# Seven-product groups of a decoder layer: common parts seeded in the accumulator banks, and four chunks in four more groups

## The chip, the cores and the metric

The kernel runs on one core of a Trainium2 chip. The metric is the device time of one execution in microseconds. A core has a matrix engine (TensorE, PE in the profile; its weight loads are PEld), a vector engine (VectorE, DVE), a scalar engine (ScalarE, ACT), GpSimd (POOL) and a sync engine (SyncE, SP) that here issues the loads of the weights. Each engine works through its own queue in order, and engines wait for one another by semaphores. Matmuls write accumulator banks in PSUM, which VectorE and ScalarE can reach as well as SBUF.

## What is computed

One decoder layer on 256 tokens with a model width of 2048, everything in float32. Three token mixers (gated linear attention, stick-breaking attention, cross-attention into 256 memory tokens) are merged by sigmoid gates, projected, and followed by a SwiGLU FFN of width 5632. Cut to what matters here:

```python
proj = rmsnorm(x, attn_norm) @ w_in              # (256, 2048) @ (2048, ...), gates among it
...
g = jax.nn.sigmoid(gates.reshape(B, T, 3, D))
merged = g[:, :, 0] * y_gla + g[:, :, 1] * y_sb + g[:, :, 2] * y_mem
x = x + merged @ w_o
h2 = rmsnorm(x, ffn_norm)
gate, up = jnp.split(h2 @ w_gate_up, 2, axis=-1)
x = x + (jax.nn.silu(gate) * up) @ w_down
```

## The kernel before

**Split numbers.** To keep float32 accuracy, every operand is held as two rounded parts, high and low. A product of a 128x128 piece of activations and a 128x512 piece of weights is three matmuls: high by high, high by low, low by high (L235, L237 and L238 in the helper `mm`, L201 to L203 in `gemm`). Activations are split once. Weights arrive as float32 blocks of four chunks (a chunk is 128 rows by 512 columns, a block 1 MB) by a load that SP issues (L229, L189), and are split two chunks at a time by `split`: ScalarE casts the high part (L136, 128x1024), VectorE subtracts it from the raw data to get the low part (L137). The pairs of high and low tiles come from rings that `widen` makes: four pairs from the start, one more before the gates, one more before the FFN, so five and then six; a split waits until the matmuls that read the pair's last contents are done. Raw blocks have three buffers and later five.

**Plain products.** `gemm` computes 256 tokens by 512 columns: for two chunks, one split and 12 matmuls (two token tiles, two chunks, three matmuls).

**Seven-product groups.** `sgemm` computes 256 tokens by two blocks of 512 columns at once, into four accumulator banks `o[t, j]` (token tile t, column block j). The first eight chunks of the contraction are two halves of four (`SP`), so operand and weights are 2x2 matrices of blocks; for the first `p` chunks of each half (p is 2 or 4) the eight block products are replaced by seven, in the Winograd form of Strassen's scheme. The weight blocks are called 11, 12 (first half, column blocks 0 and 1) and 21, 22 (second half). The sums of weight blocks are made in place in the raw buffers by VectorE (L251, two chunks at a time) just ahead of the split; the sums of operand blocks are made once per operand by `make_forms` (L356) in the background. The products are

- `p1`: block 21 into a scratch bank x0; kept (L268, ScalarE copies x0 to an SBUF piece);
- `p2`: block 11, and `p3`: block 12, each straight into one accumulator bank;
- `p5`: 21 + 22 into a second scratch bank x1;
- `p6`: into x0 on top of p1; kept; `p7`: into x0 on top of both; kept, and then two subtractions from x1 by VectorE (L303, L304) give the kept parts of the other two banks;
- `q4`: a last sum into an accumulator bank.

A product of two chunks needs one split for only 6 matmuls. What the seven products do not cover is done plainly by `rest`, two chunks at a time with 12 matmuls per split: the rest of each half (`l`, only for p = 2) and the chunks from eight on (`r0` for column block 0, `r1` for 1; four steps each with 16 chunks). At the end each bank is added to its kept part by VectorE (L346, in `result`); where the caller passes `plus` (a residual), VectorE has added that to the kept part first (L306).

The steps of a group are called in an order written out by hand (`seq`, L330 and L332); one order for groups whose operand forms come late (`late`, the first group of the gates, of w_o and of gate_up), one for the others. The tile framework then lays out every engine's queue from that program, and lets an instruction move ahead where an earlier one would still wait. `step()` lets background work (transposing results into the next operand, making forms) move on after each split.

There are 22 such groups: 4 for two of the three gates (p = 4, each followed by two plain products and a merge), 2 for w_o (p = 2), 11 for gate/up (i = 0 to 10; p = 4 for odd i, else 2) and 5 for w_down (p = 2 where n0 is 0, else 4). The FFN is done in three parts (i = 0 to 3, 4 to 7, 8 to 10): gate/up groups, then w_down groups on what they gave; in the first two parts those add their result to DRAM by a DMA that POOL issues (L1032). The last part has 12 chunks, and all but its first 1024 columns are plain products. Each gate/up group ends with an activation on ScalarE (L984) and a multiplication on VectorE (L988); its result is transposed by TensorE (L390) and split during the group behind. The forms for w_down are made during i = 2, 6 and 10.

Of the kernel before, what the change touches and what calls it, by code (L numbers as in the profile page):

```python
# [18 lines left out]
D = 2048  # L19
KD = D // P  # L20
NB = 512
# [56 lines left out]
def trunk(ctx: ExitStack, tc: tile.TileContext, a, out):  # L78
# [129 lines left out]
    def sgemm(xs, forms, w, blks, p, row0=0, late=False, plus=None):  # L208
# [36 lines left out]
        def prod(dst, left, b, last, *sums, gone=()):  # L245


            for g in range(0, p, 2):
                for to, of in sums:
                    x, y = (q[i][0][:, g : g + 2] for i in (to, of))  # L250
                    dve.tensor_tensor(x, x, y, op=ALU.add)  # L251
                wh, wl = half(q[b][0], g)
                for i in range(2):
                    mm(dst, left[g + i], wh[:, i], wl[:, i], last and g + i == p - 1)
                if g + 2 == p:
                    for i in gone:
                        q[i][1]()
                step()
# [7 lines left out]
        def keep(at):  # L266
            c[at] = piece()
            act.copy(c[at][:], x0[:])  # L268
# [5 lines left out]
        def p1():  # L274
            fetch(21, 0, SP)
            prod(x0, single(1, 0), 21, False)
            keep((0, 0))
# [5 lines left out]
        def p3(last):  # L283
            fetch(12, 1, 0)
# [40 lines left out]
        w21, w22, w11, w12 = (  # L325
            [(f,), *((rest, j, k + g) for g in range(p, SP, 2))]
            for f, j, k in ((p1, 0, SP), (p5, 1, SP), (p2, 0, 0), (p3, 1, 0))
        )
# [5 lines left out]
        todo = [into.get(f[0], [(t, f[1]) for t in range(2)] if len(f) > 1 else []) for f in seq]  # L334
        done = []
        for n, (f, *args) in enumerate(seq):
            left = {at for later in todo[n + 1 :] for at in later}
            last = [at for at in todo[n] if at not in left]
            f(*args, *([last] if args else [bool(last)] if f in into else []))
            for j in range(2):  # L340
                if j not in done and (1, 1) in c and not {(0, j), (1, j)} & left:
                    done.append(j)
# [569 lines left out]
    for b, w_br in ((1, "w_br_sb"), (0, "w_br_gla")):  # L912
        if b == 0:
            flush()
        xo = pairs((o_gla, o_sb)[b])
        for n0 in range(0, D, 2 * NB):
            gs = []
            k = (b * D + n0) // NB
            for _, result in sgemm(xs, sx, a["w_gate"], (k, k + 1), 4, late=b == 1 and n0 == 0):
                gs.append([result(t) for t in range(2)])  # L920
                for t in range(2):
                    act.activation(gs[-1][t], gs[-1][t], AF.Sigmoid, scale=r_x[:, t : t + 1])
# [21 lines left out]
    for n0 in range(0, D, 2 * NB):  # L944
# [4 lines left out]
        plus = {(t, j): xr[j][:, t] for t in range(2) for j in range(2)}  # L949
        for j, result in sgemm(ms, sm_, a["w_o"], (n0 // NB, n0 // NB + 1), 2, late=n0 == 0, plus=plus):  # L950
# [3 lines left out]
            for t in range(2):  # L954
                v = result(t, x2[:, t, n : n + NB])
# [21 lines left out]
    for part in (range(0, 4), range(4, 8), range(8, NF)):  # L977
        fs, tiles = [], []
        for i in part:
            for j, result in sgemm(hs, sf, a["w_gate_up"], (i, NF + i), 4 if i % 2 else 2, late=i == 0):  # L980
                if j == 0:
                    g = [result(t) for t in range(2)]
                    for t in range(2):
                        act.activation(g[t], g[t], AF.Silu, scale=r2[:, t : t + 1])  # L984
                    continue
                u = [result(t) for t in range(2)]
                for t in range(2):
                    dve.scalar_tensor_tensor(u[t], u[t], r2[:, t : t + 1], g[t], op0=ALU.mult, op1=ALU.mult)  # L988
# [14 lines left out]
        def stored(n, result, width=NB):  # L1003
            for t in range(2):
                for c in range(0, NB, width):
                    v = result(t, slice(c, c + width))
                    nc.sync.dma_start(out[t * P : (t + 1) * P, n + c : n + c + width], v)

        for n0 in range(0, D, 2 * NB):
            if final and n0 > 0:  # L1010
                for n in (n0, n0 + NB):
                    o = gemm(fs, a["w_down"], n, row0=4 * part[0])

                    def summed(t, cols):
                        v = x2s[t][:, n + cols.start : n + cols.stop]
                        dve.tensor_tensor(v, v, o[t][:, cols], op=ALU.add)
                        return v


                    stored(n, summed, NB // 2 if n + NB == D else NB)  # L1020
                continue
            plus = None
            if final:
                plus = {(t, j): x2s[t][:, n0 + j * NB : n0 + (j + 1) * NB] for t in range(2) for j in range(2)}
# [55 lines left out]
```

## Time and profile before

| | |
|---|---|
| median of 3 runs | 1661.63 us (1660.17 to 1662.98) |
| the profiled execution | 1660.39 us |
| its span, first to last instruction | 1658.6 us |
| instructions | 19253, of them 7398 matmul and transpose instructions on PE |
| gate/up and w_down stage | from about 956 us to the end |
| TensorE clock granted | full (1.0) in the span |

All sums are made against the profiled execution, whose own time is 1.8 us longer than its span. Busy time is a union of rows: the rows of matmuls overlap their neighbours, so a mean duration is not what one instruction takes from the engine; the distance between starts is. A timeline merges neighbouring instructions of one kind into a row with a count. In lists of waits the first name is who waited, the second who ended the wait.

### The profile page before, as it was taken

Reading aid. Unit: us, or ns where it says so; the run is one execution under the profiler, and the core shown is the slowest. Engines: PE = TensorE matmul, PEld = TensorE weight load, DVE = VectorE, ACT = ScalarE, POOL = GpSimd, SP = SyncE. Lnnn points to the kernel's source line nnn. Section 1 sums busy time; section 2 is a strip of 40 time slices with the busy share of each in tenths; the row PEclk is TensorE's granted clock in tenths of the full one; section 3 lists DMA queues with packets and bytes.
Section 4 is the critical chain, followed back from the end, with each engine's and each line's share of the span. In section 5 each row is a group of like instructions: output and inputs, shape, how many; then the busy total and the mean of one; then the engine's idle time right before and its main releaser. Section 6 shows DMA issues by size and latency. Waiting matters only on the chain.

```text
span 1658.6 us, 19253 instructions
## 1 busy us (share of the span) xinstructions
PE 1647.8 (99%) x7398; PEld 1352.2 (82%) x7398; DVE 1287.8 (78%) x1510; ACT 927.6 (56%) x1121; POOL 20.6 (1%) x32
## 2 busy tenths in 40 slices
PE   9999999999999999999999999999999999999998
PEld 7888888888877887888888888888888888888887
DVE  6756566664664669987997899997979997979984
ACT  7654454664644456555555666665656565556552
POOL 0000000000000000000000000000000000000000
PEclk9999999999999999999999999999999999999999
DMA  9765345445444557457456645565775556774572
GB/s 338 264 232 199 132 173 177 156 164 188 153 153 150 180 182 272 157 185 261 152 187 232 238 181 205 208 225 198 218 247 177 204 185 220 207 248 178 189 270 79
DMA packets 53757, 330.24 MB, mean 199 GB/s; under 512 B 5905, under 2 KB 10513, under 8 KB 15521
## 3 DMA queue, kind: packets, MB, share of 16 engines
q1 hardware_dynamic: 49968, 320.17, 54.0%
q0 software_dynamic: 3232, 8.39, 2.5%
q8 instruction: 58, 0.95, 0.2%
q10 hardware_dynamic: 464, 0.45, 0.1%
q14 instruction: 35, 0.28, 0.0%
HBM read 320.60 MB, written 8.39 MB: 198 GB/s over the span
## 4 chain that ended last, share of the span: by engine, by line
PE 94%; DVE 4%; DMA 1%; ACT 1%; issue 0%; ACTq 0%; DVEq 0%
PE acc L238 13%; PE acc L237 13%; PE acc L235 13%; PE acc L201 13%; PE acc L203 13%; PE acc L202 13%; PE tmp L237 3%; PE tmp L238 3%; PE tmp L235 3%; DVE wl L137 2%; PE tmp L390 2%; DVE raw L251 1%; DVE cv L356 1%; DMA raw<-in_w_gate_up 0%; ACT wh L136 0%; PE tmp L621 0%
## 5 line engine op out<-in xcount | busy, mean ns | idle before, releaser
L136 ACT CAST wh<-raw 128x1024 fp32r<-128x1024 f32 (+1 forms) x686 | 714.9, 1051 | 637.5 <-PE acc L203 284.5
L137 DVE TENSOR_TENSOR wl<-raw,wh 128x1024 fp32r<-128x1024 f32 (+1 forms) x686 | 824.6, 1219 | 283.6 <-ACT wh L136 278.2
L201 PE MATMUL acc<-wh,xTh 128*128 128x512 f32 x576 | 230.3, 400 | 0.0
L203 PE MATMUL acc<-wh,xTl 128*128 128x512 f32 x576 | 225.0, 391 | 0.0
L202 PE MATMUL acc<-wl,xTh 128*128 128x512 f32 x576 | 224.6, 390 | 0.0
L235 PE MATMUL acc<-wh,hh 128*128 128x512 f32 x512 | 200.0, 391 | 0.0
L238 PE MATMUL acc<-wh,hl 128*128 128x512 f32 x512 | 199.5, 390 | 0.0
L237 PE MATMUL acc<-wl,hh 128*128 128x512 f32 x512 | 199.4, 389 | 0.0
L251 DVE TENSOR_TENSOR raw<-raw 128x1024 f32<-128x1024 f32 x132 | 159.9, 1219 | 5.0 <-DMA raw<-in_w_gate_up 3.1
L203 PEld LDWEIGHTS acc<-wh,xTl 128*128 128x128 f32 x576 | 108.1, 188 | 23.4 <-issue 0.3
L201 PE MATMUL acc<-wh,oh 128*128 128x512 f32 x320 | 126.1, 396 | 0.8 <-ACT oh L139 0.8
L201 PEld LDWEIGHTS acc<-wh,xTh 128*128 128x128 f32 x576 | 108.3, 188 | 22.0 <-issue 1.4
L202 PE MATMUL acc<-wl,oh 128*128 128x512 f32 x320 | 125.7, 393 | 0.5 <-DVE wl L137 0.5
L202 PEld LDWEIGHTS acc<-wl,xTh 128*128 128x128 f32 x576 | 108.3, 188 | 21.7 <-issue 0.7
L203 PE MATMUL acc<-wh,ol 128*128 128x512 f32 x320 | 125.5, 392 | 0.0
L237 PEld LDWEIGHTS acc<-wl,hh 128*128 128x128 f32 x512 | 96.2, 188 | 20.1 <-DVE wl L137 0.3
L238 PEld LDWEIGHTS acc<-wh,hl 128*128 128x128 f32 x512 | 96.1, 188 | 20.0
L235 PEld LDWEIGHTS acc<-wh,hh 128*128 128x128 f32 x512 | 96.2, 188 | 19.6
L235 PE MATMUL acc<-wh,fh 128*128 128x512 f32 x220 | 85.9, 391 | 0.1
L237 PE MATMUL acc<-wl,fh 128*128 128x512 f32 x220 | 85.6, 389 | 0.0
L238 PE MATMUL acc<-wh,fl 128*128 128x512 f32 x220 | 85.5, 389 | 0.0
L201 PEld LDWEIGHTS acc<-wh,oh 128*128 128x128 f32 x320 | 60.6, 189 | 15.5 <-ACT oh L139 1.7
(291 smaller groups left out, 2203.7 us busy)
## 6 DMA issues: line engine op xcount, KB each, us to landing
raw<-in_w_gate_up SPq DMA_DIRECT2D x88, 1024.0 KB, 5.0
raw<-in_w_in SPq DMA_DIRECT2D x72, 1024.0 KB, 4.9
raw<-in_w_down SPq DMA_DIRECT2D x44, 1024.0 KB, 4.9
raw<-in_w_gate SPq DMA_DIRECT2D x32, 1024.0 KB, 4.9
raw<-in_w_o SPq DMA_DIRECT2D x16, 1024.0 KB, 4.9
raw<-in_w_mem_kv SPq DMA_DIRECT2D x15, 1024.0 KB, 5.0
raw<-in_w_br_mem SPq DMA_DIRECT2D x8, 1024.0 KB, 5.1
raw<-in_w_br_sb SPq DMA_DIRECT2D x8, 1024.0 KB, 6.9
```

The costliest lines, as they stand in the source:

```text
L136: act.copy(hi, src)
L137: dve.tensor_tensor(lo, src, hi.bitcast(F32), op=ALU.subtract)
L201: pe.matmul(o[t][:], xh[:, s], wh[:, j], start=k == 0, stop=False)
L202: pe.matmul(o[t][:], xh[:, s], wl[:, j], start=False, stop=False)
L203: pe.matmul(o[t][:], xl[:, s], wh[:, j], start=False, stop=k == nk - 1)
L235: pe.matmul(dst[:], xh, wh, start=id(dst) not in begun, stop=False, skip_group_check=True)
L237: pe.matmul(dst[:], xh, wl, start=False, stop=False, skip_group_check=True)
L238: pe.matmul(dst[:], xl, wh, start=False, stop=last, skip_group_check=True)
L251: dve.tensor_tensor(x, x, y, op=ALU.add)
L356: dve.tensor_tensor(dst, a, b, op=op)
L390: pe.transpose(dst, src, ident)
```

## The change

The scratch bank's running sums are no longer kept in SBUF and added at the end. In groups that are not late, `put` writes each common part straight into its accumulator bank (ScalarE copies x0, or VectorE subtracts x0 from a copy of p5), marks the bank as begun, and the later matmuls add onto it; `result` then returns the bank itself, and the caller's activation, multiplication or addition reads it there. Late groups keep SBUF pieces and the addition. The residual is no longer passed in; the caller adds it to the result. The order outside the late groups becomes p1, p5, p6, p2, p7, p3, the plain pairs of blocks 22 and 12, q4, those of 21 and 11, then `r0` and `r1`; block sums change so that 12 stays untouched (p6 uses 21 + 22 + 12, made in block 21's buffer; q4 adds that to block 11), and block 21's buffer is held until q4. Four chunks are used for i = 1, 3, 4, 5, 7, 8 and 9 of gate/up, and for all w_down groups but the last part's. The core of the diff:

```diff
-        def keep(at):
-            c[at] = piece()
-            act.copy(c[at][:], x0[:])
+        def put(at, *src):
+
+            if late:
+                c[at] = piece()
+                dst = c[at][:]
+            else:
+                dst = o[at][:]
+                begun.add(id(o[at]))
+            if len(src) == 1:
+                act.copy(dst, src[0][:])
+            else:
+                dve.tensor_tensor(dst, src[0][:], src[1][:], op=ALU.subtract)
...
         def p1():
             fetch(21, 0, SP)
             prod(x0, single(1, 0), 21, False)
-            keep((0, 0))
+            put((0, 0), x0)
...
         def q4(last):
-            prod(o[1, 0], single(0, 1), 11, last, (11, 12), gone=(11, 12))
+            prod(o[1, 0], single(0, 1), 11, last, (11, 21))
...
         def p5():
             fetch(22, 1, SP)
             prod(x1, formed(1), 21, True, (21, 22))
+            c["p5"] = piece()
+            act.copy(c["p5"][:], x1[:])
...
-            prod(x0, formed(2), 12, False, (22, 12), (12, 21), gone=(21,))
-            keep((0, 1))
+            if 12 not in q:
+                fetch(12, 1, 0)
+            prod(x0, formed(2), 21, False, (22, 12), (21, 12))
+            put((0, 1), c["p5"], x0)
...
         def p7():
-            prod(x0, formed(3), 22, True, gone=(22,))
-            keep((1, 0))
-            c[1, 1] = piece()
-            dve.tensor_tensor(c[1, 1][:], x1[:], c[1, 0][:], op=ALU.subtract)
-            dve.tensor_tensor(c[0, 1][:], x1[:], c[0, 1][:], op=ALU.subtract)
-            for at, more in (plus or {}).items():
-                dve.tensor_tensor(c[at][:], c[at][:], more, op=ALU.add)
+            prod(x0, formed(3), 22, True)
+            put((1, 0), x0)
+            put((1, 1), c["p5"], x0)
...
+        a, b, e, f, g, h, i = ((x,) for x in (p1, p2, p3, q4, p5, p6, p7))
         if late:
-            seq = [*w21, *w11, *r0[:2], *r1[:2], *w22, *w12, *r0[2:3], (p6,), *r0[3:], (p7,), (q4,), *r1[2:]]
+            seq = [a, *l21, b, *l11, *r0[:2], *r1[:2], g, *l22, e, *l12, *r0[2:3], h, *r0[3:], i, f, *r1[2:]]
         else:
-            seq = [*w21, *r0[:1], *w22, *r0[1:2], *w12, *r0[2:3], (p6,), *r0[3:], *w11, (p7,), *r1[:1], (q4,), *r1[1:]]
+            seq = [a, g, h, b, i, e, *l22, *l12, f, *l21, *l11, *r0, *r1]
...
-                    def result(t, dst=None, cols=slice(0, NB), j=j):
-                        d = c[t, j][:] if dst is None else dst
-                        dve.tensor_tensor(d[:, cols], o[t, j][:, cols], c[t, j][:, cols], op=ALU.add)
-                        return d[:, cols]
+                    def result(t, j=j):
+                        if late:
+                            dve.tensor_tensor(c[t, j][:], o[t, j][:], c[t, j][:], op=ALU.add)
+                            return c[t, j][:]
+                        return o[t, j][:]
...
-                v = result(t, x2[:, t, n : n + NB])
+                v = x2[:, t, n : n + NB]
+                dve.tensor_tensor(v, result(t), xr[j][:, t], op=ALU.add)
...
-            for j, result in sgemm(hs, sf, a["w_gate_up"], (i, NF + i), 4 if i % 2 else 2, late=i == 0):
+            for j, result in sgemm(hs, sf, a["w_gate_up"], (i, NF + i), 2 if i % 4 == 2 or i == 0 else 4, late=i == 0):
                 if j == 0:
-                    g = [result(t) for t in range(2)]
+                    g = [piece()[:] for t in range(2)]
                     for t in range(2):
-                        act.activation(g[t], g[t], AF.Silu, scale=r2[:, t : t + 1])
+                        act.activation(g[t], result(t), AF.Silu, scale=r2[:, t : t + 1])
                     continue
-                u = [result(t) for t in range(2)]
+                u = [piece()[:] for t in range(2)]
                 for t in range(2):
-                    dve.scalar_tensor_tensor(u[t], u[t], r2[:, t : t + 1], g[t], op0=ALU.mult, op1=ALU.mult)
+                    dve.scalar_tensor_tensor(u[t], result(t), r2[:, t : t + 1], g[t], op0=ALU.mult, op1=ALU.mult)
...
-            for j, result in sgemm(fs, sd, a["w_down"], blks, 4 if n0 else 2, row0=4 * part[0], plus=plus):
+            for j, result in sgemm(fs, sd, a["w_down"], blks, 2 if final else 4, row0=4 * part[0]):
                 n = n0 + j * NB
                 if final:
-                    stored(n, lambda t, cols: result(t, cols=cols))
+                    stored(n, result)
                     continue
                 for t in range(2):
-                    nc.gpsimd.dma_start(x2d[:, t, n : n + NB], result(t), accum_op=ALU.add)
+                    v = piece()
+                    act.copy(v[:], result(t))
+                    nc.gpsimd.dma_start(x2d[:, t, n : n + NB], v[:], accum_op=ALU.add)
```

The gates' caller changes as gate/up's does, and `stored` adds the result to the residual in `x2s` before it stores it.

## Rows read from the trace of the kernel before

**Rows 1.** The page's first part: busy time, share of the span, instructions.

```profile
PE 1647.8 (99%) x7398; PEld 1352.2 (82%) x7398; DVE 1287.8 (78%) x1510; ACT 927.6 (56%) x1121; POOL 20.6 (1%) x32
```

**Rows 2.** The page's fourth part: the chain that ended last, by engine.

```profile
PE 94%; DVE 4%; DMA 1%; ACT 1%; issue 0%; ACTq 0%; DVEq 0%
```

**Rows 3.** Timeline of PE in a w_down group: start, duration; first and thirty-first matmul.

```profile
1134.25 0.39 PE L235 MATMUL acc<-wh,fh 128*128 128x512 f32 x1
...
1141.05 0.39 PE L235 MATMUL acc<-wh,fh 128*128 128x512 f32 x1
```

**Rows 4.** Windows (us, then busy by engine: PE, PEld, DVE, ACT, POOL): i = 2, i = 3.

```profile
1040.23:1083.35 43.12, 43.12 (x195) 35.69 (x194) 42.06 (x48) 26.07 (x32) 0.00 (x0) 1.00 0.55 197
1083.35:1125.12 41.77, 41.77 (x190) 34.58 (x188) 40.94 (x41) 26.58 (x29) 0.00 (x0) 1.00 0.55 201
```

**Rows 5.** List of waits, 1040 to 1593 us: total, times, longest; four of 13 rows.

```profile
POOL x2d L1032 <- DVE cv L346: 492.6, 12, 197.6
ACT wh L136 <- PE acc L238: 162.2, 146, 3.5
...
DVE wl L137 <- ACT wh L136: 52.7, 63, 1.5
ACT wh L136 <- DVE raw L251: 22.4, 12, 4.1
```

**Rows 6.** Groups of instructions by line: count, busy us, mean ns, idle before.

```profile
L346 DVE TENSOR_TENSOR cv<-acc,cv 128x512 f32<-128x512 f32 x80 | 53.4, 682 | 0.1
L268 ACT COPY cv<-tmp 128x512 f32<-128x512 f32 x66 | 38.5, 583 | 12.3 <-PE tmp L238 12.1
L984 ACT ACTIVATE cv<-cv,r 128x512 f32<-128x512 f32 x22 | 15.9, 723 | 2.3 <-DVE cv L346 2.2
L303 DVE TENSOR_TENSOR cv<-tmp,cv 128x512 f32<-128x512 f32 x22 | 15.0, 683 | 1.3 <-ACT cv L268 1.3
L346 DVE TENSOR_TENSOR x<-acc,cv 128x512 f32<-128x512 f32 x8 | 5.5, 682 | 0.4 <-PE acc L238 0.4
L306 DVE TENSOR_TENSOR cv<-cv,xr 128x512 f32<-128x512 f32 x8 | 5.1, 683 | 0.0
L306 DVE TENSOR_TENSOR cv<-cv,x2s 128x512 f32<-128x512 f32 x4 | 2.6, 682 | 0.0
```

**Rows 7.** Timeline of DVE: weight sums, splits, two subtractions, two multiplications.

```profile
1010.48 4.62 DVE L251 TENSOR_TENSOR raw<-raw 128x1024 f32<-128x1024 f32 x4
1015.02 9.16 DVE L137 TENSOR_TENSOR wl<-raw,wh 128x1024 fp32r<-128x1024 f32 x8
...
1157.08 0.68 DVE L303 TENSOR_TENSOR cv<-tmp,cv 128x512 f32<-128x512 f32 x1
1157.68 0.68 DVE L304 TENSOR_TENSOR cv<-tmp,cv 128x512 f32<-128x512 f32 x1
...
1252.24 1.40 DVE L988 SCALAR_TENSOR_TENSOR cv<-cv,r 128x512 f32<-128x512 f32 x2
```

**Rows 8.** Timeline of ACT: idle before an instruction, and by whom, in brackets.

```profile
998.12 1.05 ACT L136 CAST wh<-raw 128x1024 fp32r<-128x1024 f32 x1 [1.61 <-PE acc L238]
...
1148.05 0.59 ACT L268 COPY cv<-tmp 128x512 f32<-128x512 f32 x1 [0.30 <-PE tmp L238]
1148.53 1.05 ACT L136 CAST wh<-raw 128x1024 fp32r<-128x1024 f32 x1
```

**Rows 9.** Issues of the block loads: count, KB each, median us to landing.

```profile
raw<-in_w_gate_up SPq DMA_DIRECT2D x88, 1024.0 KB, 5.0
```

**Rows 10.** Window of the first, late group of the gates; columns as in rows 4.

```profile
605.53:645.94 40.41, 36.72 (x161) 28.22 (x160) 40.41 (x49) 25.24 (x33) 0.00 (x0) 1.00 0.51 177
```

**Rows 11.** Timeline of PE in that group: four stalls between 633.8 and 640 us.

```profile
635.09 0.50 PE L237 MATMUL tmp<-wl,sxh 128*128 128x512 f32 x1 [0.91 <-DVE wl L137]
...
637.36 0.49 PE L235 MATMUL tmp<-wh,sxh 128*128 128x512 f32 x1 [0.84 <-ACT wh L136]
638.31 0.73 PE L235 MATMUL acc<-wh,xTh 128*128 128x512 f32 x2 [0.45 <-ACT wh L136]
639.63 0.50 PE L237 MATMUL tmp<-wl,sxh 128*128 128x512 f32 x1 [0.59 <-DVE wl L137]
```

More of the change, by code (lines that the diff above doesn't have):

```diff
@@ L206, in gemm, with sgemm @@
         return o
-    def sgemm(xs, forms, w, blks, p, row0=0, late=False, plus=None):
+    def sgemm(xs, forms, w, blks, p, row0=0, late=False):
         nk = len(xs)
@@ L243, in half, with prod @@
             return wh, wl
-        def prod(dst, left, b, last, *sums, gone=()):
+        def prod(dst, left, b, last, *sums):
             for g in range(0, p, 2):
@@ L254, in prod @@
                     mm(dst, left[g + i], wh[:, i], wl[:, i], last and g + i == p - 1)
-                if g + 2 == p:
-                    for i in gone:
-                        q[i][1]()
                 step()
@@ L331, in sgemm @@
         else:
-            seq = [*w21, *r0[:1], *w22, *r0[1:2], *w12, *r0[2:3], (p6,), *r0[3:], *w11, (p7,), *r1[:1], (q4,), *r1[1:]]
+            seq = [a, g, h, b, i, e, *l22, *l12, f, *l21, *l11, *r0, *r1]
+        uses = {21: [a, g, h, f, *l21], 22: [g, h, i, *l22], 11: [b, f, *l11], 12: [h, e, *l12]}
         into = {p2: [(0, 0)], p3: [(0, 1)], q4: [(1, 0)]}
-        todo = [into.get(f[0], [(t, f[1]) for t in range(2)] if len(f) > 1 else []) for f in seq]
-        done = []
-        for n, (f, *args) in enumerate(seq):
+        todo = [into.get(x[0], [(t, x[1]) for t in range(2)] if len(x) > 1 else []) for x in seq]
@@ L337, in sgemm @@
+        gone = []
+        for n, (what, *args) in enumerate(seq):
             left = {at for later in todo[n + 1 :] for at in later}
             last = [at for at in todo[n] if at not in left]
-            f(*args, *([last] if args else [bool(last)] if f in into else []))
+            what(*args, *([last] if args else [bool(last)] if what in into else []))
+            for x, by in uses.items():
+                if (what, *args) in by and not any(y in by for y in seq[n + 1 :]):
+                    q[x][1]()
@@ L340, in sgemm @@
             for j in range(2):
-                if j not in done and (1, 1) in c and not {(0, j), (1, j)} & left:
-                    done.append(j)
-                    def result(t, dst=None, cols=slice(0, NB), j=j):
-                        d = c[t, j][:] if dst is None else dst
-                        dve.tensor_tensor(d[:, cols], o[t, j][:, cols], c[t, j][:, cols], op=ALU.add)
-                        return d[:, cols]
+                if j not in gone and (p7,) not in seq[n + 1 :] and not {(0, j), (1, j)} & left:
+                    gone.append(j)
+                    def result(t, j=j):
[3 more added lines that the diff above has]
+                        return o[t, j][:]
@@ L919, in trunk @@
             for _, result in sgemm(xs, sx, a["w_gate"], (k, k + 1), 4, late=b == 1 and n0 == 0):
-                gs.append([result(t) for t in range(2)])
+                gs.append([piece()[:] for t in range(2)])
                 for t in range(2):
-                    act.activation(gs[-1][t], gs[-1][t], AF.Sigmoid, scale=r_x[:, t : t + 1])
+                    act.activation(gs[-1][t], result(t), AF.Sigmoid, scale=r_x[:, t : t + 1])
             if b == 0 and n0 > 0:
@@ L948, in trunk @@
             nc.sync.dma_start(xr[-1][:], a["x"][:, n : n + NB].rearrange("(t p) n -> p t n", p=P))
-        plus = {(t, j): xr[j][:, t] for t in range(2) for j in range(2)}
-        for j, result in sgemm(ms, sm_, a["w_o"], (n0 // NB, n0 // NB + 1), 2, late=n0 == 0, plus=plus):
+        for j, result in sgemm(ms, sm_, a["w_o"], (n0 // NB, n0 // NB + 1), 2, late=n0 == 0):
             if x2 is None:
@@ L1005, in stored @@
                 for c in range(0, NB, width):
-                    v = result(t, slice(c, c + width))
+                    v = x2s[t][:, n + c : n + c + width]
+                    dve.tensor_tensor(v, v, result(t)[:, c : c + width], op=ALU.add)
                     nc.sync.dma_start(out[t * P : (t + 1) * P, n + c : n + c + width], v)
@@ L1012, in trunk @@
                     o = gemm(fs, a["w_down"], n, row0=4 * part[0])
[L1014 to L1020, printed above, removed]
+                    stored(n, lambda t: o[t], NB // 2 if n + NB == D else NB)
                 continue
[L1022 to L1024 removed]
             blks = (n0 // NB, n0 // NB + 1)
[L1026 removed]
+            for j, result in sgemm(fs, sd, a["w_down"], blks, 2 if final else 4, row0=4 * part[0]):
                 n = n0 + j * NB
                 if final:
[L1029 removed]
+                    stored(n, result)
                     continue
                 for t in range(2):
[L1032 removed]
+                    v = piece()
+                    act.copy(v[:], result(t))
+                    nc.gpsimd.dma_start(x2d[:, t, n : n + NB], v[:], accum_op=ALU.add)
 def kernel(**inputs):
```

8 lines of the change are left out of this document (4 added, 4 removed).

## The prediction

> **What bounds the kernel now.** I read the busy line first: TensorE's matmul rows fill 99% of the span, VectorE 78%, ScalarE 56% [rows 1]. The chain that ended last says that the 99% is a bound and not an appearance: 94% of it is PE, and DVE and ACT have 5% between them [rows 2]. Then the price of a matmul. Its row says 390 ns, but the rows overlap: between 1134.25 and 1141.05 us thirty matmuls start, 6.80 / 30 = 0.227 us apart [rows 3]. That spacing is what one matmul more or less is worth, and two whole groups of the gate/up product bear it out: the group with two chunks in the seven products (i = 2) takes 43.12 us and the next, with four (i = 3), 41.77 us, with 6 matmuls fewer: 1.35 us, or 0.225 each [rows 4]. The same rows show the danger: VectorE is busy 42.06 and 40.94 us of the two, 98%. Yet in the list of waits from 1040 to 1593 us no row has PE as the one that waits; ScalarE waits for TensorE to give back operand buffers, 146 times, 162.2 us [rows 5]. So the split weights are ahead of TensorE there, as far as the six buffer pairs allow.
>
> **Fewer matmuls.** Six per group that goes from two chunks to four: seven products of 2 chunks and four pairs done plainly are 42 + 48 = 90 matmuls, seven products of 4 chunks 84. Such groups are i = 4, i = 8 and the first w_down group of the first two parts: 4 x 6 = 24 matmuls, 24 x 0.227 = **-5.45 us**. They lie on the path, as PE waits for nothing there.
>
> **VectorE's work.** Gone are 88 adds of an accumulator to its kept part and 12 of the residual to that part (counts 80 + 8, and 8 + 4) [rows 6]. Back come 12 adds in the three late groups and 12 that add the residual (8 in w_o, 4 in the last w_down). The two subtractions per group stay (44). Net -76 at 0.60 us, the spacing of two neighbours of that size [rows 7], is -45.6 us. The four changed groups add 16 weight sums and 12 splits; eight splits in a row take 9.16 us, the last of them its own 1.22, so one costs (9.16 - 1.22) / 7 = 1.13 us [rows 7]: 28 x 1.13 = +31.6 us. VectorE ends 14 us lighter. It is not what PE waits for, so I book it at nothing. ScalarE gets 12 splits of 1.05 [rows 8] and, in w_down, 16 copies of 0.58 [rows 6]: 22 us more on an engine at 56%; nothing.
>
> **The order: seven products first.** This is the part that can cost. Outside the late groups the products were spread between plain pairs, each of which gives TensorE 12 matmuls (2.72 us) per split; now they follow one another, and a product gives 6 (1.36 us) per split while VectorE pays 1.13 for the split and 1.13 more for each weight sum. A walk through a four-chunk gate/up group, T = 0 at its first matmul: six pairs (4 + 1 + 1 in the code's rings) mean that its first split may start when the third of the eight plain pairs of the group before is through, T = -5 x 2.72 = -13.6; after 0.3 and ScalarE's 1.05 [rows 8], VectorE can go on from -12.25. The second half of the last product, q4, is wanted at T = 13 x 1.36 + 0.23 = 17.9. That leaves 30.2 us. VectorE must do 14 splits and 8 sums (24.9), the two subtractions (1.2), and from the group before two multiplications (1.4 for both [rows 7]) and two small splits (1.2): 28.7 us. It fits by 1.5 us, of which about 0.5 goes in waits for a buffer, if the sums run as soon as their blocks are there; the trace shows that they do, four in a row ahead of their splits at 1010.48 us [rows 7]. If each sum ran only before its own split, q4 would come 1.2 us late. So 0 to 1.2 us for each of 14 groups; I take 0 for the eleven of the FFN, and 0.1 for the three of the gates, which have five pairs and so 2.7 us less lead, but a plain product before them: **+0.3**.
>
> The first group behind the late gate/up one (i = 1) starts with less lead, as the late order ends in one plain pair, two products and two plain pairs: first split at -10.9 instead of -13.6, so up to 2.5 us late by the same walk. At 998.12 us, at its start, ScalarE was waiting 1.61 us for TensorE to free a pair [rows 8], so the lead was full; I take 0.
>
> In the groups i = 2, 6 and 10 VectorE also makes the next product's operand forms (12 operations of 0.60, eight of them in front of the last split of block 12). Counted the same way up to there: 8 splits and 4 sums 13.6, forms 4.8, multiplications, small splits and subtractions 3.8, so 22.2 of 23.4 us, with about 2 us lost to waits for a buffer: 0 to 1.0 late each. I take 0.17 each, **+0.5**, since sums done early fill such waits.
>
> **The hand-over in the banks.** New waits for PE: p6 adds to x0 once ScalarE has copied it to bank (0,0), and p7 once VectorE has taken p5 - x0 for bank (0,1). What queues behind p6 or p7 is all of PE. With four chunks another product lies between, 2.72 us, and both fit. With two chunks it is 1.36 us. A copy waits 0.30 us for the end of its product and the next instruction starts 0.48 later [rows 8]: under 1.36. The subtraction needs 0.3 + 0.68 if VectorE is free, and up to 1.13 more if it is inside a sum or split: 0 to 0.8 late. Five groups have two chunks and the new order: I take 0.2 each, **+1.0**. No row has a write into a bank by these engines; the nearest are the same copy and subtraction into SBUF [rows 6], 583 and 683 ns, and I use these.
>
> **At nothing.** Activations and multiplications read the bank itself; a bank is next wanted by the following group's put, 2.7 us in at the earliest, against 0.72 for the read. The block loads on the SP queue stay eight per group of 16 chunks, 5.0 us each [rows 9], and move past nothing; block 21 is now held until q4. The buffer that q4 frees at T = 17 has its block by 22; its first split comes at 40.8 - 13.6 = 27.2, so 5 us of cover; without it the whole load would show. The x2d transfers on POOL wait for a copy of 0.58 instead of an add of 0.68. One more piece per group, five of eight, is read out before its turn. The late groups keep their order, sums and PE work; the tail is the same.
>
> **Sum:** -5.45 + 0.3 + 0.5 + 1.0 = **-3.65 us**. The profiled execution took 1660.39 us (span 1658.6 and 1.8 around it), so 1656.7 beside it; the median of the runs is 1661.63, 1.24 above, so **1658.0 us**, -0.22%. All lower bounds (no loss) give 1656.2, all upper ones (14 x 1.2 + 2.5 + 3 + 4) give 1682.
>
> **Rivals.** (a) *The products-first order starves TensorE; slower.* Place: the second half of q4 in the four-chunk groups. Price: 1.2 us x 14 = 16.8, so 1661.63 - 5.45 + 16.8 = 1673. It decides once a group loses over 5.45 / 14 = 0.39 us. For it: the margin of 1.0 us in 30 is thin, and the one group in which VectorE is behind already, the first gate group at 605.53 to 645.94, has PE busy 36.72 of 40.41 us [rows 10], with stalls of 0.91, 0.84, 0.45 and 0.59 us in six [rows 11]. Against: VectorE has 2.4 us less to do in each group than now.
> (b) *The small losses eat the gain; no change.* Hand-overs 5 x 0.8 and i = 1 at 1.0 instead of the values above: 4.0 + 0.3 + 0.5 + 1.0 = 5.8, so 1662. For it: VectorE is inside some instruction 98% of the time. Against: its order is laid so that such steps come in time now; copies waited at most 0.3.
> (c) *VectorE is the bound; much faster.* If TensorE had room and VectorE's 98% set the pace of the groups, its 14 us would come off: 1647.6. Against it stands the list without one PE wait [rows 5]. The Trainium skill (Perfetto Trace Analysis, Identifying the Most-Contended Engine) says to judge TensorE by the busy share of its weight loads and not of its matmuls, which is 82% here: by that VectorE would be the tighter engine in these groups, and the sum would be -14. This trace disagrees: six matmuls fewer gave back 1.35 us between two groups in which VectorE was equally busy.
>
> **Chances.** Forecast 0.45, (a) 0.24, (b) 0.28, (c) 0.03. About 0.2%, 3.3 us, is what this kernel's measurement can tell from no change. Faster: forecast and (c), 0.48; same 0.28; slower 0.24. The likeliest case alone reaches from 1655 to 1659.5. For 8 in 10 the range runs from 1655 (no loss, and 1.2 of scatter as in the runs before) through (b) to 1670, into (a) where half of its groups pay; that leaves out (c) and the far part of (a).
>
> **What would show it.** Right: 7374 matmul rows, 24 fewer; spacing still 0.227; i = 4 and i = 8 near 41.8 us instead of 43.1; no PE wait of over 0.3 us on wl between 1040 and the end; VectorE near 1274 us, its 128x512 adds nearly gone. Wrong: PE waiting for wl before q4's matmuls or the first plain pair in every group (a); PE waiting for the subtraction before p7 in the two-chunk groups (b); four-chunk groups well under 41 us (c).

## The result and the profile after

The changed kernel takes **1677.2 us** (median; 1676.24 to 1678.01) against 1661.99 for the kernel before on the same chip: 1.0093 times as long, interval 1.0075 to 1.011. So it is 15.2 us slower, and the time lies above the range of the prediction. The profiled execution took 1676.24 us, its span is 1674.5, 15.9 more than before.

The page's busy line and the chain by engine:

```profile
PE 1649.8 (99%) x7374; PEld 1345.9 (80%) x7374; DVE 1274.0 (76%) x1462; ACT 941.4 (56%) x1149; POOL 20.7 (1%) x32
...
PE 90%; DVE 8%; issue 1%; ACT 1%; DMA 1%; DVEq 0%; ACTq 0%
```

and the groups of instructions by line that answer to [rows 6] (a bank as target is `acc`; line numbers are those of the kernel after):

```profile
L276 DVE TENSOR_TENSOR acc<-cv,tmp 128x512 f32<-128x512 f32 x38 | 26.2, 688 | 3.3 <-ACT acc L274 3.3
L274 ACT COPY acc<-tmp 128x512 f32<-128x512 f32 x38 | 21.7, 571 | 43.2 <-PE tmp L241 43.2
...
L303 ACT COPY cv<-tmp 128x512 f32<-128x512 f32 x22 | 13.0, 590 | 8.8 <-PE tmp L241 8.0
L359 DVE TENSOR_TENSOR cv<-acc,cv 128x512 f32<-128x512 f32 x12 | 8.1, 685 | 0.0
```

The result's addition is left in the three late groups alone (L359, 12 instead of 88), and 19 groups write two copies and two subtractions into banks, at 571 and 688 ns, as good as into SBUF (583 and 683). The counts are as forecast: 7374 matmul rows, 24 fewer, and VectorE at 1274.0 us, 14 lighter [rows 1]. The share of PE is the same 99%, yet the chain has 8% on VectorE where it had 4 [rows 2]: 90% of the chain on PE still leaves a place where PE waits. The busy share doesn't show it; windows of equal length do. Columns: the window, its length, then busy us and rows of PE, PEld, DVE, ACT, POOL; granted clock, DMA share, GB/s. First after, then before:

```profile
675.00:850.00 175.00, 168.91 (x731) 135.96 (x730) 136.29 (x132) 95.75 (x104) 0.00 (x0) 0.99 0.52 192
...
900.00:950.00 50.00, 48.06 (x216) 38.60 (x215) 41.93 (x47) 30.55 (x43) 2.33 (x4) 1.00 0.75 272
...
1000.00:1060.00 60.00, 56.49 (x246) 44.73 (x245) 54.35 (x53) 35.35 (x39) 0.00 (x0) 1.00 0.53 210
1060.00:1600.00 540.00, 539.25 (x2411) 445.30 (x2410) 484.34 (x464) 334.87 (x379) 14.92 (x18) 1.00 0.59 214
```

```profile
675.00:850.00 175.00, 175.00 (x781) 144.89 (x780) 154.56 (x160) 104.38 (x114) 0.00 (x0) 1.00 0.57 204
900.00:950.00 50.00, 50.00 (x230) 41.41 (x229) 44.26 (x52) 31.77 (x47) 3.40 (x6) 1.00 0.73 251
1000.00:1060.00 60.00, 59.84 (x271) 48.81 (x270) 59.79 (x65) 37.39 (x45) 0.00 (x0) 1.00 0.49 176
```

From 675 to 850 us, where the three products-first groups of the gates lie, TensorE gets through 50 rows fewer: 50 x 0.227 = 11.4 us. From 900 to 950 (the second w_o group) it is 14, 3.2 us, and from 1000 to 1060 (i = 1) 25, 5.7 us. Taken matmul by matmul, the distances between starts beyond 0.227 us add up to about 43 us after and 22 before: of the 20.9 more, 11.4 lie in the gates, 2.7 in the second w_o group, 4.7 in i = 1, and only 1.5 in all of the FFN behind it. 20.9 - 5.45 for the 24 matmuls is 15.5, against 15.9 in the spans. **So the FFN behind i = 1, where most of the changed groups are, went as forecast, and the five groups ahead of that point did not.**

In the list of waits PE and its weight loads now appear as who waits; four of the rows from 600 to 1060 us (total, times, longest). Some 6.3 us of these 26 belong to the late group up to 646 us, which stalls in the kernel before as well [rows 11]; from 660 to 1060 us the kernel before has no such row of over 0.5 us in all:

```profile
PEld tmp L238 <- ACT wh L136: 7.8, 6, 1.6
...
PEld acc L238 <- ACT wh L136: 6.3, 11, 0.8
PEld tmp L240 <- DVE wl L137: 6.2, 7, 1.7
PEld acc L240 <- DVE wl L137: 5.7, 8, 1.1
```

and from 1070 to 1600 us, after i = 1, the two that are left beside ScalarE's wait for free pairs (before: [rows 5]):

```profile
ACT wh L136 <- PE acc L241: 113.9, 89, 2.1
...
PEld acc L240 <- DVE wl L137: 2.2, 4, 0.7
...
PE acc L240 <- DVE wl L137: 0.7, 3, 0.2
```

Next, **one group of the gates from near by.** Its first matmul (p1) is at 676.54 us; p5 starts at 679.26, p6 at 681.98, and p6's second half is due at 683.34. The timeline of PE and that of VectorE (a count of 2 is two neighbours in one row; brackets: idle before, and by whom):

```profile
683.11 0.39 PE L241 MATMUL tmp<-wh,sxl 128*128 128x512 f32 x1
684.71 0.49 PE L238 MATMUL tmp<-wh,sxh 128*128 128x512 f32 x1 [1.21 <-ACT wh L136]
685.65 0.49 PE L238 MATMUL acc<-wh,xTh 128*128 128x512 f32 x1 [0.45 <-ACT wh L136]
686.16 0.50 PE L240 MATMUL tmp<-wl,sxh 128*128 128x512 f32 x1
```

```profile
664.27 1.23 DVE L137 TENSOR_TENSOR wl<-raw,wh 128x1024 fp32r<-128x1024 f32 x1 [1.50 <-ACT wh L136]
665.41 1.28 DVE L900 TENSOR_TENSOR cv<-acc,cv 128x512 f32<-128x512 f32 x2
666.61 1.28 DVE L901 TENSOR_TENSOR merged<-merged,cv 128x512 f32<-128x512 f32 x2
...
673.62 2.35 DVE L253 TENSOR_TENSOR raw<-raw 128x1024 f32<-128x1024 f32 x2
675.89 0.68 DVE L900 TENSOR_TENSOR cv<-acc,cv 128x512 f32<-128x512 f32 x1
...
680.56 2.35 DVE L253 TENSOR_TENSOR raw<-raw 128x1024 f32<-128x1024 f32 x2
683.74 4.63 DVE L137 TENSOR_TENSOR wl<-raw,wh 128x1024 fp32r<-128x1024 f32 x4 [0.83 <-ACT wh L136]
```

Before its split at 664.27 VectorE is idle for 1.50 us, waiting for ScalarE, which waits for TensorE to give back a pair: the lead is full. From 665.41 to 682.91 VectorE has no gap. It does 8 merge steps (4.8 us), 6 weight sums and 5 splits, 4.8 + 11 x 1.14 = 17.3 us. The two sums that p6's second half needs come last, from 680.56 to 682.91. ScalarE's next casts follow p5's copy from 682.66 on; by the times, p6's second half takes the second of them and starts at 684.71, 1.37 us late, with the rest of it waiting for its low part until 686.16. The other two gate groups stall in the same way, 1.21 and 0.45 us idle at 752.13 and 753.08 and again at 819.90 and 820.85, and all three once more, by about 0.6 us, at q4 (698.06, 763.90 and 831.7). Yet over 40.9 us, about the length of a group, VectorE is busy only 83%:

```profile
672.50:713.40 40.90, 38.76 (x161) 30.79 (x160) 33.75 (x34) 22.98 (x25) 0.00 (x0) 0.96 0.50 186
```

In i = 1, whose first matmul is at 1013.01 us, the stalls stand at p6 (3.1 us beyond the spacing in all, the first row) and at q4 (1.7, the second):

```profile
1021.02 0.50 PE L240 MATMUL tmp<-wl,sfh 128*128 128x512 f32 x1 [1.25 <-DVE wl L137]
...
1035.23 0.50 PE L240 MATMUL acc<-wl,hh 128*128 128x512 f32 x1 [0.76 <-DVE wl L137]
```

### The profile page after: what moved, and what is told of

It reads as the page before. It is cut to its first block, busy times and chain, and to the rows that moved or that the text cites. A ratio compares the mean times of both kernels' runs of the same rounds, so it can differ in the third digit from the quotient of the medians.

```text
span 1674.5 us, 19186 instructions
## 1 busy us (share of the span) xinstructions
PE 1649.8 (99%) x7374; PEld 1345.9 (80%) x7374; DVE 1274.0 (76%) x1462; ACT 941.4 (56%) x1149; POOL 20.7 (1%) x32
## 4 chain that ended last, share of the span: by engine, by line
PE 90%; DVE 8%; issue 1%; ACT 1%; DMA 1%; DVEq 0%; ACTq 0%
PE acc L201 13%; PE acc L202 13%; PE acc L203 13%; PE acc L240 13%; PE acc L241 12%; PE acc L238 12%; DVE wl L137 4%; PE tmp L240 3%; PE tmp L241 3%; PE tmp L238 3%; PE tmp L404 1%; DVE raw L253 1%; DVE cv L370 1%; ACT wh L136 1%; DMA raw<-in_w_mem_kv 0%
## 5 line engine op out<-in xcount | busy, mean ns | idle before, releaser
L137 DVE TENSOR_TENSOR wl<-raw,wh 128x1024 fp32r<-128x1024 f32 (+1 forms) x698 | 833.6, 1219 | 310.1 <-ACT wh L136 307.5
L240 PE MATMUL acc<-wl,hh 128*128 128x512 f32 x488 | 190.2, 390 | 1.7 <-DVE wl L137 1.7
L238 PE MATMUL acc<-wh,hh 128*128 128x512 f32 x488 | 189.8, 391 | 0.5 <-ACT wh L136 0.4
L241 PE MATMUL acc<-wh,hl 128*128 128x512 f32 x488 | 189.6, 389 | 0.0
L253 DVE TENSOR_TENSOR raw<-raw 128x1024 f32<-128x1024 f32 x148 | 178.9, 1220 | 4.9 <-DMA raw<-in_w_gate_up 1.8
L240 PEld LDWEIGHTS acc<-wl,hh 128*128 128x128 f32 x488 | 91.6, 188 | 22.8 <-DVE wl L137 3.8
L238 PEld LDWEIGHTS acc<-wh,hh 128*128 128x128 f32 x488 | 91.6, 188 | 20.5 <-ACT wh L136 1.6
L238 PE MATMUL acc<-wh,fh 128*128 128x512 f32 x196 | 76.2, 390 | 0.0
L240 PE MATMUL acc<-wl,fh 128*128 128x512 f32 x196 | 76.1, 389 | 0.0
L241 PE MATMUL acc<-wh,fl 128*128 128x512 f32 x196 | 76.1, 389 | 0.0
```

The lines of the kernel that those rows point to most:

```text
L137: dve.tensor_tensor(lo, src, hi.bitcast(F32), op=ALU.subtract)
L238: pe.matmul(dst[:], xh, wh, start=id(dst) not in begun, stop=False, skip_group_check=True)
L240: pe.matmul(dst[:], xh, wl, start=False, stop=False, skip_group_check=True)
L241: pe.matmul(dst[:], xl, wh, start=False, stop=last, skip_group_check=True)
```

## The experiments

Diffs against the kernel after are marked A, those against the kernel before B. Times are medians, or one run where "one run" is said; the kernel before on the same chip took 1660.34 to 1662.67.

**1. The chunk counts alone** (B: the old order and SBUF pieces with the new counts).

```diff
-            for j, result in sgemm(hs, sf, a["w_gate_up"], (i, NF + i), 4 if i % 2 else 2, late=i == 0):
+            for j, result in sgemm(hs, sf, a["w_gate_up"], (i, NF + i), 2 if i % 4 == 2 or i == 0 else 4, late=i == 0):
...
-            for j, result in sgemm(fs, sd, a["w_down"], blks, 4 if n0 else 2, row0=4 * part[0], plus=plus):
+            for j, result in sgemm(fs, sd, a["w_down"], blks, 2 if final else 4, row0=4 * part[0], plus=plus):
```

> The kernel before with nothing but the four groups (i = 4, i = 8, the first w_down group of parts one and two) taken from two chunks to four; parts are kept in SBUF, order spread. Theory O (the products-first order is what costs): 24 matmuls x 0.227 = 5.45 us less, so 1656.5 against 1662.0 before, as the spread order hides VectorE's work in the other four-chunk groups already. Rival V (VectorE, 98% busy in these groups, has no room for 28 more operations of 1.13 us): no gain or up to 8 us slower, 1662 to 1670, with PE waiting for wl in the four groups.

Measured: 1656.15 us (1655.08 to 1658.38), ratio 0.9966 (0.9954 to 0.9979): 6.5 us faster, and faster than both kernels. Its page and the stages:

```profile
PE 1641.0 (99%) x7374; PEld 1347.4 (81%) x7374; DVE 1317.2 (80%) x1538; ACT 939.7 (57%) x1133; POOL 20.5 (1%) x32
```

```profile
675.00:850.00 175.00, 175.00 (x781) 144.89 (x780) 154.56 (x159) 104.36 (x114) 0.00 (x0) 1.00 0.56 201
900.00:950.00 50.00, 50.00 (x230) 41.40 (x229) 44.07 (x52) 32.31 (x48) 3.40 (x6) 1.00 0.73 253
1000.00:1060.00 60.00, 60.00 (x274) 49.53 (x273) 59.78 (x65) 37.40 (x45) 0.00 (x0) 1.00 0.49 176
```

VectorE is 29 us busier than before, and from 660 us on PE and its weight loads have no wait of over 0.5 us: the 24 matmuls are worth what was booked, and VectorE's total is not what bounds.

**2. The seeding and its order alone** (A: the old chunk counts).

> The changed kernel with the chunk counts of before: seeding and order alone. Theory O, with the loss in the gates, the second w_o group and i = 1 as the trace of after has it (none of them among the four groups): 1677.2 + 5.45 = 1682.6 us. Rival N (every products-first group with four chunks loses 1 us or more): the four groups lose less with two chunks, so 1678 or below.

Measured: 1683.72 us (1681.75 to 1689.62), ratio 1.0136 (1.0115 to 1.0158). That is 6.5 above the kernel after, as much as the counts give in experiment 1. The two parts of the change add up: about -6.5 and +21.

**3. The three gate groups without seeding** (A), one run; `seed=False` keeps SBUF pieces and takes the spread order:

```diff
-            if late:
+            if late or not seed:
...
+        elif seed:
+            seq = [a, g, h, b, i, e, *l22, *l12, f, *l21, *l11, *r0, *r1]
         else:
-            seq = [a, g, h, b, i, e, *l22, *l12, f, *l21, *l11, *r0, *r1]
+            seq = [a, *l21, *r0[:1], g, *l22, *r0[1:2], e, *l12, *r0[2:3], h, *r0[3:], b, *l11, i, *r1[:1], f, *r1[1:]]
...
-                        if late:
+                        if late or not seed:
```

("The run before this one" in the expectation is experiment 9 here.)

> As the run before this one, but only the gates' three groups go back to SBUF pieces and the spread order. Theory O: 11 us less than after, about 1666; w_o and i = 1 keep their 7. If the gates' stalls come from something other than seeding and order (a slower load, the clock), the time stays near 1677.

Measured: 1666.63 us. The loss of the gates is gone with the seeding and its order (782 rows from 675 to 850 us), and w_o and i = 1 keep theirs (216 and 245 rows in their windows).

**4. The weight sums left out in these three groups** (A), one run: `for to, of in sums if sums_on else ():`.

> The changed kernel with the sums of weight blocks left out in the gates' three products-first groups (their products then use the plain blocks): VectorE has 8 x 1.13 = 9 us less to do in each, ScalarE's copies out of the scratch banks still wait for the end of their products. Theory L (VectorE's burst is longer than the lead that five pairs give): the gates' 11 us of extra idle go, about 1666. Theory Q (ScalarE's copies wait at the head of its queue with the next splits behind them): the idle stays, 1674 to 1677.

Measured: 1665.46 us.

**5. Only p6's four sums left out there** (A), one run.

> The changed kernel without the four sums of weight blocks in front of p6, in the gates' three products-first groups alone (p6 then uses block 21 + 22); the sums for p5 and q4 stay. If the binding deadline is p6's second half, where TensorE stalls for 1.4 + 0.7 + 0.3 us in the trace of after and in the mixed run, 4 x 1.13 = 4.5 us less in front of it take nearly all 11 us of the gates' idle away, half-clock stretches included: 1666 to 1668. If it is the second half of q4, as the prediction had it, the stalls at p6 stay and the time is 1674 or more.

Measured: 1665.59 us, the same. The window of the gates, in 4 and in 5:

```profile
675.00:850.00 175.00, 175.00 (x781) 144.90 (x780) 122.10 (x120) 102.73 (x111) 0.00 (x0) 1.00 0.57 204
```

```profile
675.00:850.00 175.00, 175.00 (x781) 144.53 (x780) 132.16 (x130) 101.77 (x111) 0.00 (x0) 1.00 0.55 204
```

All 50 rows are back, with the order and the hand-over through the banks as in the kernel after. 3 x 4 x 1.13 = 13.6 us less on VectorE, at the right place, is enough. The expectation meant this to tell p6 from q4, which it can't: p6's sums lie ahead of both. The timeline tells that: PE stalls at p6 first.

**6. ScalarE's copies in the gates don't wait** (A), one run: they read an SBUF tile instead of the scratch bank, so that no cast is queued behind a copy that waits for TensorE.

```diff
-                act.copy(dst, src[0][:])
+                act.copy(dst, src[0][:] if other is None else other)
...
-            act.copy(c["p5"][:], x1[:])
+            act.copy(c["p5"][:], x1[:] if other is None else other)
```

> The changed kernel, but in the gates' three products-first groups ScalarE's three copies read another SBUF tile (merged) instead of the scratch banks, so they no longer wait for a product; VectorE's work and the two subtractions stay. Theory Q: the 11 us go, about 1666. Theory L: they stay, 1674 to 1677.

Measured: 1677.21 us, no gain.

```profile
675.00:850.00 175.00, 170.36 (x744) 137.30 (x743) 137.63 (x134) 95.43 (x103) 0.00 (x0) 1.00 0.53 194
900.00:950.00 50.00, 48.32 (x211) 38.93 (x210) 40.53 (x47) 30.16 (x42) 2.32 (x4) 0.97 0.73 267
1000.00:1060.00 60.00, 56.80 (x235) 44.74 (x234) 52.83 (x52) 34.87 (x39) 0.00 (x0) 0.94 0.51 199
```

The gates got 13 rows of the 50 back (3 us), and the two later places lost 16, where the granted clock is now below 1. The stall at p6 stays, 0.73 and 0.45 us idle at 684.66 and 685.61, 0.48 us less than in the kernel after. Three times that is 1.4 of the 3 us; the other 1.6 are the first group's, which keeps the full clock here (see the last section). So the copies in ScalarE's queue are a small part. The casts still wait for TensorE to give back pairs: ScalarE is idle for 4.34 us before 682.61.

**7. The lead: five pairs in the FFN instead of six**, in the kernel after and, **8.**, in the kernel before; one run each.

```diff
-    widen("ring3", 0, 1)
```

> The changed kernel without the sixth pair of split tiles in the FFN, five there as in the gates. Theory L: the eleven four-chunk groups of the FFN then lose as the gates do, 2 to 4 us each: 1700 to 1720. Theory Q: the copies wait no longer than with six, at most 5 us more: 1677 to 1682.

> The kernel before without the sixth pair, as the measure for the run above. Spread order: a plain pair between products gives VectorE its time back, so both theories expect little: 1662 to 1666.

Measured: 1707.12 and 1661.86 us. From 1050 to 1600 us, in 7 and in 8:

```profile
1050.00:1600.00 550.00, 534.59 (x2346) 432.83 (x2344) 470.02 (x449) 326.74 (x370) 14.77 (x18) 1.00 0.55 195
```

```profile
1050.00:1600.00 550.00, 549.90 (x2460) 454.75 (x2459) 492.70 (x494) 323.58 (x355) 14.86 (x18) 1.00 0.62 212
```

One pair less costs the products-first order 30 us and the spread order nothing. The gates have five pairs too. That a sixth would cure them follows from this and from the sums below; no run gave them one.

**9. Gates, w_o and i = 1 without seeding, the rest as in the kernel after** (A, 3 with two more callers).

> The changed kernel, but the groups of the gates, the second of w_o and i = 1 keep their parts in SBUF pieces, add them at the end and run in the spread order; the rest of the FFN is seeded and runs products first, with the new chunk counts. Theory O local to those five groups: their extra PE idle (about 11 in the gates, 2.5 in w_o, 5 at i = 1) goes, 1677.2 - 18.5 = 1658.7, range 1656.5 to 1660. Rival N: the FFN's own groups pay too, above 1665.

Measured: 1669.89 us (1669.79 to 1670.58), ratio 1.0048 (1.0033 to 1.0063): 11 us above what was expected.

```profile
675.00:850.00 175.00, 175.00 (x781) 144.89 (x780) 150.90 (x152) 103.24 (x110) 0.00 (x0) 1.00 0.57 205
900.00:950.00 50.00, 50.00 (x230) 41.39 (x230) 43.49 (x50) 31.87 (x45) 2.86 (x5) 1.00 0.75 262
1028.00:1072.00 44.00, 36.70 (x145) 28.02 (x144) 42.02 (x48) 26.22 (x32) 0.00 (x0) 0.92 0.53 195
```

The gates and w_o are clean, and i = 2 now pays about 12 us: it has become the first products-first group behind one that adds its results on VectorE. There VectorE is busy 42.02 of 44 us, and PE 36.70, part of it at a lower clock. So a loss goes with the passage from one kind of group to the other, and not with i = 1 alone. It isn't the passage by itself: the stalls begin at p7 (2.21 us at 1052.02, waiting for wl), where VectorE also makes the operand forms that i = 2 has and i = 1 has not, and no run parts the two.

**10. i = 1 with two chunks** (A), one run.

> The changed kernel with two chunks instead of four for i = 1, the first group behind a late one in the FFN. Theory L: 7 operations of 1.13 us fewer in that group's burst, so its 4.9 us of extra idle fall to 1.5 or less, at 1.4 us more of matmuls: about 1675. If the idle there were the late group's own work or a load, it stays, and the time is 1678 to 1679.

Measured: 1673.91 us. i = 1 is clean: 271 rows from 1000 to 1060 us instead of 246. With two chunks its burst ahead of p6 is half as long (3 splits and 3 sums, 6.8 us).

**11. Seeding kept, plain pairs drawn forward between the last products** (A).

```diff
-            seq = [a, g, h, b, i, e, *l22, *l12, f, *l21, *l11, *r0, *r1]
+            seq = [a, g, h, b, i, *l21, *r0[:1], e, *l22, *r0[1:2], *l12, f, *l11, *r0[2:], *r1]
```

> The changed kernel with seeding everywhere and its chunk counts, but outside the late groups only the five products that the seeds need stand in a row (p1, p5, p6, p2, p7); p3 and q4 are put between plain pairs. Theory L (the burst against the lead): by the end of p7 VectorE needs 16 operations of 1.13 instead of 22 by the end of q4, and TensorE reaches that point 5.4 us earlier, so a group is about 1.5 to 2.5 us less late; the gates keep some 4 of 11 us, w_o and i = 1 half of theirs: about 1667, range 1662 to 1670. Theory S (seeding itself, its writes into and reads from the banks, costs): little change, 1673 to 1677.

Measured: 1672.01 us (1671.69 to 1673.58), ratio 1.0061 (1.0044 to 1.0078): 5 us gained where 10 were expected. The window of the gates:

```profile
675.00:850.00 175.00, 170.00 (x735) 138.10 (x734) 137.95 (x133) 96.77 (x104) 0.00 (x0) 0.98 0.52 192
```

This eases q4 and leaves p1, p5, p6, p2, p7 together. The stalls at q4 are gone, about 0.6 us in each gate group and 1.7 in i = 1, and the FFN behind i = 1 gets 7 rows more. Those at p6 stay (in the first group 1.21 and 0.45 us at 685.21 and 686.15). The gates got only 4 of their 50 rows back, as the third group now has a stretch at half clock (0.50 from 820.4 to 823 us).

**12. One step beyond experiment 1: four chunks in the second w_o group too** (B, with 1).

> The kernel before with the new chunk counts, and four chunks for the second w_o group too; spread order, parts in SBUF. VectorE is busy 77 of 96 us around the w_o groups, so 7 more operations of 1.13 fit there: 6 matmuls fewer, 1.4 us less than the run with the new chunk counts alone, 1654.8; no change or more if the w_o group, with five pairs, runs out of lead even in the spread order.

Measured: 1659.25 us (1657.66 to 1662.2), ratio 0.9985 (0.9976 to 0.9995): better than before, 3 worse than experiment 1. The group stalls even in the spread order (1.21 us at 930.10, waiting for wl), with five pairs and a late group ahead of it, and the stage from 1000 us on has 9 rows fewer than in experiment 1:

```profile
900.00:950.00 50.00, 48.31 (x219) 39.20 (x219) 48.71 (x57) 32.41 (x48) 3.40 (x6) 1.00 0.63 215
1000.00:1060.00 60.00, 58.54 (x265) 47.87 (x264) 59.73 (x64) 37.74 (x44) 0.00 (x0) 1.00 0.50 177
```

So experiment 1 is the best of all versions measured.

## Why the prediction was wrong

- **Fewer matmuls, -5.45: right.** -6.5 in experiment 1, with an interval that holds -5.45, and 6.5 between the kernel after and experiment 2. Spacing stayed 0.227.
- **VectorE's work, nothing: right as a total.** 1274.0 us, as counted, and the total decides nothing; where in a group the work lies does (experiments 4 and 5). Rival (c) falls: experiment 1 has VectorE at 80% and is the fastest, the kernel after has it at 76% and is 21 us slower. The Trainium skill's rule that the busy share of the weight loads judges TensorE (Perfetto Trace Analysis, Identifying the Most-Contended Engine) would let 81% in experiment 1 pass as room; no PE wait of over 0.5 us from 1040 us on says that there was none.
- **Hand-overs +1.0, forms +0.5: right in the sum, by luck.** All the FFN behind i = 1 lost 1.5 us more than before. But PE has no wait for a hand-over: the subtraction waits 1.6 us in all for ScalarE's copy from 1070 us on, and PE not for it. What PE waits for is a late split, 0.41 us at 1077.07, 1327.60 and 1578.14, once in each of i = 2, 6 and 10, the groups that make forms. So the hand-overs cost nothing that a trace shows, and the forms about 1.2 us.
- **The FFN's four-chunk groups other than i = 1, nothing: right.** i = 2 and i = 3:

```profile
1060.31:1103.97 43.66, 43.41 (x195) 35.62 (x194) 39.30 (x43) 25.57 (x30) 0.00 (x0) 1.00 0.52 193
1103.97:1145.71 41.74, 41.74 (x189) 34.58 (x188) 38.45 (x37) 26.04 (x29) 0.00 (x0) 1.00 0.52 201
```

The second row is i = 3 (41.77 before [rows 4]); the first, i = 2, is the one that shows the small loss.

- **The step that failed: "0.1 for the three of the gates", and "I take 0" for i = 1.** Measured 11.4 and 4.7 us; the second w_o group, which had only its share of a hand-over, lost 2.7. The walk to q4 was made for six pairs and not made again for these groups. For the gates the text named the pair that lacks and the plain product before them, and let the second cancel the first; it did not count the merge that this plain product leaves to VectorE. With five pairs VectorE has 30.2 - 2.7 = 27.5 us up to q4 for 24.9 + 1.2 and the merge. All eight merge steps (4.8) would make that 3.4 us late; the 3.3 us of them that the trace has behind the start of that lead (T = -9.6) make it 1.9. Measured are 2.4 us at p6 and 0.6 at q4 in each group, and 1.6 in the first for a lower clock. For i = 1 the start at -10.9 was right (ScalarE's cast is at 1002.33, T = -10.7), and the same walk, with the late group's four result additions (2.4), is 24.9 + 1.2 + 2.6 + 2.4 = 31.1 in 27.5 us: 3.6 late, for 4.7 measured.
- **The walk also looked at one deadline only.** p6's second half is wanted at T = 5 x 1.36 + 0.23 = 7.0, and 6 of the 8 sums and 6 of the 14 splits, 12 x 1.13 = 13.6 us, lie ahead of it. With six pairs VectorE has from -12.25 to 7.0 = 19.3, less 2.6 for the group before: 3 us to spare, and 1.5 at q4, so the FFN is clean. With five it has 16.6 for the same 13.6 and the merge. In the group above the first split starts at 667.81 behind four merge steps, T = -8.7, four more (2.4) fall into the burst, and the last sum ends at 682.91, T = 6.4, with a cast of 1.05 and a split of 1.13 still to come: 1.6 late before anything queues. For i = 1 it is 13.6 + 2.4 + 2.6 in 16.6: 2 short. So p6 takes most of the loss first, and q4 adds the rest.
- **The second w_o group** is another case of the same. Between 914.79 and 928.63 us VectorE has, besides three weight sums and four splits, six additions, a subtraction and three small splits of the late group ahead, some 5.4 us. PE waits 0.64 us for such a small split at 926.12 and 0.87 for p6's split at 928.69.
- **The row that was taken as proof of a full lead at i = 1**, ScalarE waiting 1.61 us at 998.12 [rows 8], is from the spread order, 0.25 us behind the first matmul of the group there (997.87). In the kernel after ScalarE last waits for a pair 8 us before the group's first matmul, and then for a weight sum:

```profile
1005.05 1.06 ACT L136 CAST wh<-raw 128x1024 fp32r<-128x1024 f32 x1 [1.66 <-PE acc L241]
...
1011.63 1.05 ACT L136 CAST wh<-raw 128x1024 fp32r<-128x1024 f32 x1 [0.92 <-DVE raw L253]
```

- **Rival (a)** had the sign and the mechanism. Its price (16.8 for 20.9 measured) came near by luck, as the place was wrong: not q4 in all 14 four-chunk groups but p6 first, and q4 behind it, in five groups with a short lead, one of them of two chunks. Its evidence from [rows 10] and [rows 11] was the better guide: that first gate group has five pairs too.
- The seeding itself costs no time that a run shows. It costs through the order: a bank must be written before its first matmul, so the products that make the common parts go first. Experiments 4 and 5 keep that order and lose nothing, given VectorE's time; experiment 11 shows that the place of p3 and q4 is the smaller part.

Of the gates' 11.4 us the lower clock (below) is 1.6. Open: which of the two would cure the gates by itself, a sixth pair or no merge ahead, and why experiment 9 pays 12 us in i = 2 where i = 1 paid 4.7.

## What to carry to other kernels

For a burst of work that runs ahead through a ring of buffers, make the sum for every group that has another lead or other work on the producer's queue, and for every deadline in it, not only the last: what the producer must have done by then against the lead (buffers times the time each is held) less what else is on its queue. A share of 83% over the length of a group hid a starved TensorE, and one pair more or less decided 30 us. When a change has a cheap part and a part that fixes the order, time them apart: here the chunk counts alone were the gain.

## Unexpected of the hardware

A stall can cost twice. In the gate group above the granted clock goes to 0.50, the 1.2 GHz level, after 4.1 us in which PE is busy 2.43, while it is already busy again:

```profile
676.50:683.10 6.60, 6.60 (x30) 5.45 (x30) 6.41 (x8) 2.55 (x4) 0.00 (x0) 1.00 0.00 0
683.10:687.20 4.10, 2.43 (x8) 1.23 (x7) 3.46 (x4) 4.10 (x5) 0.00 (x0) 0.99 0.00 0
687.20:690.20 3.00, 3.00 (x8) 2.27 (x7) 3.00 (x5) 1.52 (x3) 0.00 (x0) 0.50 0.00 0
```

Matmuls are then 0.427 us apart instead of 0.227; 8 rows in 3.00 us cost 8 x 0.2 = 1.6 us. The two gate groups behind it have the same stalls at p6, and from 691 to 850 us the granted clock is 1.00. The kernel before has a stall of the same kind that kept the full clock too:

```profile
633.00:637.00 4.00, 2.62 (x11) 1.49 (x9) 4.00 (x4) 1.25 (x2) 0.00 (x0) 1.00 0.37 119
637.00:640.00 3.00, 1.59 (x5) 0.80 (x6) 3.00 (x4) 3.00 (x4) 0.00 (x0) 1.00 0.90 314
```

No run here tells what makes the difference. Such stretches go with the rows that experiment 6 gained in one stage and lost in two others (0.97 and 0.94), and with rows that moved where an edit did not reach: the kernel of experiment 7 has 0.97 and 211 rows from 900 to 950 us, ahead of the stage that it changes, for 1.00 and 216 in the kernel after. So a single run can differ by 1 to 2 us for this alone.
